# A decoder trunk's MLP on one core: the first product as seven half-size products per block instead of eight

## The chip, the core and the metric

The kernel runs on one core of a Trainium2 chip. A time is the time of one execution on the device in microseconds (us), the median of several runs. Engines are named as in the profile: PE does matrix products, PEld loads their weights, DVE and ACT are the vector and scalar engines, POOL a slower third one, and SP issues the transfers (DMA) between DRAM and the on-chip memory.

## The reference: what is computed

One layer of a decoder trunk on 512 tokens with 2048 features: three parallel token mixers, merged by gates, an output projection, and an MLP. Only the last part matters here.

```python
D_MODEL = 2048; SEQ = 512; D_FF = 4 * D_MODEL
x = x + merged @ w_out                       # output projection, residual
h = rmsnorm(x, norm_mlp)                     # y * rsqrt(mean(x*x) + 1e-6) * g
x = x + jnp.square(jax.nn.relu(h @ mlp_w1)) @ mlp_w2   # (512 x 2048)(2048 x 8192), then (512 x 8192)(8192 x 2048)
out = rmsnorm(x, final_norm)
```

All products are wanted with the accuracy of 32-bit floats.

## The kernel before

Activations lie feature-major: a tile has 128 features on the partitions and the 512 tokens along the row. Each operand of a big product is split into a high and a low part (`hl`: ACT rounds a copy to the type fp32r, DVE subtracts it), and a product of two tiles is three matrix instructions: high by high, high by low, low by high. `gemm` does one output tile of 128 features: it calls `wtiles` for each slab of up to eight weight tiles (128 x 1024 numbers, 512 KB), which issues the load, ACT's cast and DVE's subtraction; raw slabs have 3 buffers (`wraw`), high and low parts 3 each (`whl`), and a slab's high and low parts are free again when PE has used the slab.

The order on PE is that of the code; the other engines and the queue SP are ordered by a scheduler, and each works its list strictly in order. Everything is read as one stream on PE:

- the mixers and the gates, up to 1471 us of the trace;
- the output projection `wo`: 16 output tiles, each 16 weight tiles x 3 instructions. For each, DVE adds the product to the residual `x1`, and ACT and DVE make `hh` and `ho`, the scaled high and low parts that the first MLP product reads;
- the MLP in 8 rounds `c`. A round makes 8 output tiles of the first product (`w1_{f}`, 16 weight tiles x 3 instructions of 512 columns each), whose result goes through ReLU, the factor `R` (one over the rms) and a square into `ah`, `al`; then 16 output tiles of the second product over these 8 tiles (`w2_{c}_{j}`, 8 x 3 instructions), each added to `x1[j]` by DVE;
- the last eight tiles of the last round are done in two halves of the tokens, in instructions of 256 columns, and the final norm follows for each half.

The psum banks of these products are a ring of two (`gps`, tag "g", `gb = 2`): the third product begins when the first one's bank has been read. Products into other banks use a ring of six (`ps`).

## Time and profile before

| | |
|---|---|
| median of 3 runs | 3062.77 us (3061.63 to 3068.74) |
| profiled execution | span 3059.8 us, first to last instruction; its own time is not listed beside it, and the span lies 2.97 below the median of the runs |
| PE busy | 3001.3 us, 98% of the span |
| DVE, ACT, POOL busy | 1557.3, 989.0, 336.8 us |
| data moved | 370.72 MB, mean 121 GB/s |
| `wo`, first to last instruction | 1471.7 to 1645.5 us |
| MLP up to the halves of the tokens | 1645.7 to 2995.6 us |

"Busy" of PE counts each matrix instruction from its start to its end, and these overlap, so the mean length of an instruction is not what one costs in a stream: that is the distance between the starts of neighbours. Idle time is that just before an instruction, with what released it.

### The profile page before, as it was taken

The page shows a single profiled execution, that of the slowest core. Times are in us where ns is not written, and L with a number is a line of the kernel's source. Part 1 is how long each engine was busy: PE and PEld are TensorE (multiplying, and loading weights), DVE is VectorE, ACT ScalarE, POOL GpSimd, SP SyncE. Part 2 cuts the span into 40 slices and gives each one's busy share as a digit, 9 for nine tenths or more (in the row PEclk, how much of TensorE's full clock was granted, in tenths as well). Part 3 has the DMA queues.
Part 4 walks back from the last instruction along what each step waited for, and adds up shares of the span by engine and source line. Part 5 has one row for each costly group of instructions (what it writes and reads, how often), then busy time and mean ns, then how long its engine had stood idle before and what let it go on. Part 6 is the DMA issues. An engine that isn't in the chain of part 4 may idle for free.

```text
span 3059.8 us, 36455 instructions
## 1 busy us (share of the span) xinstructions
PE 3001.3 (98%) x14143; PEld 2468.2 (81%) x14143; DVE 1557.3 (51%) x2350; ACT 989.0 (32%) x1224; POOL 336.8 (11%) x572
## 2 busy tenths in 40 slices
PE   8999988999999999999999999999999999999997
PEld 7888776788877777888888888888888888888887
DVE  7766888855664555555334334333333434333335
ACT  6554121234662233422223222122222212222235
POOL 1001766530000000011110000000000000000003
PEclk9999988999999999999999999999999999999999
DMA  5345333445337163655432333333233323323334
GB/s 181 124 162 185 114 103 98 136 131 166 102 103 190 55 186 97 229 165 170 157 98 94 97 99 96 99 98 97 97 97 97 97 96 97 97 96 97 97 97 151
DMA packets 172638, 370.72 MB, mean 121 GB/s; under 512 B 63377, under 2 KB 74385, under 8 KB 171665
## 3 DMA queue, kind: packets, MB, share of 16 engines
q1 hardware_dynamic: 172464, 368.38, 38.2%
q8 instruction: 112, 1.84, 0.3%
q14 instruction: 62, 0.50, 0.1%
HBM read 318.81 MB, written 44.58 MB: 119 GB/s over the span
## 4 chain that ended last, share of the span: by engine, by line
PE 85%; DVE 6%; POOL 3%; DMA 3%; SPq 1%; issue 1%; ACT 0%; DVEq 0%; ACTq 0%; POOLq 0%
PE w L748 15%; PE w L749 15%; PE w L750 15%; PE gt L748 5%; PE gt L750 5%; PE gt L749 5%; PE z L748 2%; PE z L750 2%; PE z L749 2%; PE wo L750 2%; PE up L748 2%; PE wo L748 2%; PE up L750 2%; PE up L749 2%; PE wo L749 2%
## 5 line engine op out<-in xcount | busy, mean ns | idle before, releaser
L731 ACT CAST whw<-wrw 128x1024 fp32r<-128x1024 f32 x264 | 278.0, 1053 | 885.8 <-PE w L749 872.4
L32 DVE TENSOR_TENSOR wlw<-wrw,whw 128x1024 fp32r<-128x1024 f32 x264 | 324.1, 1227 | 405.2 <-ACT whw L731 405.2
L748 PE MATMUL w<-ah,whw 128*128 128x512 f32 (+1 forms) x1088 | 409.9, 377 | 0.1
L750 PE MATMUL w<-ah,wlw 128*128 128x512 f32 (+1 forms) x1088 | 409.7, 377 | 0.0
L749 PE MATMUL w<-al,whw 128*128 128x512 f32 (+1 forms) x1088 | 409.7, 377 | 0.0
L748 PE MATMUL w<-hh,whw 128*128 128x512 f32 x1024 | 398.7, 389 | 0.0
L750 PE MATMUL w<-hh,wlw 128*128 128x512 f32 x1024 | 398.4, 389 | 0.0
L749 PE MATMUL w<-ho,whw 128*128 128x512 f32 x1024 | 398.4, 389 | 0.0
L748 PE MATMUL gt<-uh,whgt 128*128 128x512 f32 x768 | 310.6, 404 | 2.8 <-DVE gz L26 2.8
L750 PE MATMUL gt<-uh,wlgt 128*128 128x512 f32 x768 | 300.6, 391 | 2.0 <-DVE wlgt L32 2.0
L749 PE MATMUL gt<-ul,whgt 128*128 128x512 f32 x768 | 300.2, 391 | 0.0
L29 DVE TENSOR_TENSOR x<-x,w 128x512 f32<-128x512 f32 (+1 forms) x136 | 89.2, 656 | 388.0 <-PE w L750 388.0
L748 PE MATMUL z<-uh,whin 128*128 128x512 f32 x608 | 243.7, 401 | 11.8 <-DVE zs L26 11.8
L750 PE MATMUL z<-uh,wlin 128*128 128x512 f32 x608 | 241.0, 396 | 8.1 <-DVE wlin L32 8.1
L749 PE MATMUL z<-ul,whin 128*128 128x512 f32 x608 | 240.0, 395 | 0.0
L748 PEld LDWEIGHTS w<-ah,whw 128*128 128x128 f32 x1088 | 204.7, 188 | 37.7 <-issue 0.2
L749 PEld LDWEIGHTS w<-al,whw 128*128 128x128 f32 x1088 | 204.7, 188 | 37.5
L750 PEld LDWEIGHTS w<-ah,wlw 128*128 128x128 f32 x1088 | 204.7, 188 | 37.4
L748 PEld LDWEIGHTS w<-hh,whw 128*128 128x128 f32 x1024 | 192.2, 188 | 40.2 <-issue 0.2
L749 PEld LDWEIGHTS w<-ho,whw 128*128 128x128 f32 x1024 | 192.2, 188 | 40.1 <-issue 0.2
L750 PEld LDWEIGHTS w<-hh,wlw 128*128 128x128 f32 x1024 | 192.2, 188 | 39.9
L29 POOL TENSOR_TENSOR acc<-acc,sq 128x512 f32<-128x512 f32 x29 | 49.7, 1713 | 1521.7 <-ACT sq L830 1490.7
(442 smaller groups left out, 4577.8 us busy)
## 6 DMA issues: line engine op xcount, KB each, us to landing
wrw<-in_w SPq DMA_DIRECT2D x264, 512.0 KB, 3.6
wrgt<-in_w_in SPq DMA_DIRECT2D x96, 512.0 KB, 4.0
wrin<-in_w_in SPq DMA_DIRECT2D x76, 512.0 KB, 3.6
wrup<-in_w_up SPq DMA_DIRECT2D x32, 512.0 KB, 4.0
wrwo<-in_w_out SPq DMA_DIRECT2D x32, 512.0 KB, 3.6
gd<-gz SPq DMA_DIRECT2D x48, 256.0 KB, 2.2
gl<-gd SPq DMA_DIRECT2D x48, 256.0 KB, 3.1
zd<-zs SPq DMA_DIRECT2D x21, 256.0 KB, 2.0
```

Of the source, the lines that this page charges most:

```text
L29: (eng or self.nc.vector).tensor_tensor(out, a, b, ALU.add)
L32: (eng or self.nc.vector).tensor_tensor(out, a, b, ALU.subtract)
L731: nc.scalar.copy(hi, raw)
L748: nc.tensor.matmul(ps, hi[:, ws], xh, start=first, stop=False)
L749: nc.tensor.matmul(ps, hi[:, ws], xl, start=False, stop=False)
L750: nc.tensor.matmul(ps, lo[:, ws], xh, start=False, stop=last)
```

## The change

The first MLP product is cut in 32 units `u` of 256 output features, and each unit is a 2 x 2 block product: two halves of the 2048 input features (8 tiles each), two output tiles, two halves of the tokens (256). Of such a block product the change computes seven products of sums instead of eight (the Strassen-Winograd form): each of the seven is 8 weight tiles x 3 instructions of 256 columns. Their inputs are sums of the two feature halves and the two token halves, made once and kept per product (`hA` for products 1, 5, 6, 3, made by `hsums` while `wo` runs; three more, `hB`, that go to DRAM as `d3` and are read back and split at the start of the first unit). The weights' sums are made per unit by `wsums`: 5 loads of 512 KB, 4 additions on DVE, and a cast and a subtraction for each of the 7. `w1_out` copies three partial results from psum, makes the four quarters of the block, applies ReLU, square and the factor, and stores the 512 KB to DRAM (`hid`). The second product is as before, but it begins after the last unit, reads its activations back (`hidden`), and takes `x1` from DRAM too (`x1d`, stored during `wo`). `R2` is now 1/(mean + 1e-6), multiplied after the square.

```diff
+    ORDER = (1, 5, 6, 3, 7, 2, 4)
+    BANK = {1: "a", 6: "a", 7: "a", 4: "a", 5: "c", 3: "c", 2: "b"}
...
+    def wsums(self, name, B, pool):
+        nc = self.nc
+        at = {}
+        def load(c, q):
+            p = pool if c == "A" else None
+            at[c] = (p or self.wp).tile([P, 1024], F32, name=f"w{c}{name}", tag="wA" if p else "wraw", bufs=self.wA if p else self.wraw)
+            nc.sync.dma_start(at[c], B[q])
+            return at[c]
+        def acc(c, t):
+            self.add(at[c], at[c], t)
+            return at[c]
+        how = {1: lambda: load("A", "11"), 5: lambda: acc("A", load("D", "12")), 6: lambda: acc("A", load("B", "22")),
+               3: lambda: at["B"], 7: lambda: acc("B", load("E", "12")), 2: lambda: load("C", "21"), 4: lambda: acc("A", at["C"])}
+        for i in self.ORDER:
+            with self.tc.high_priority(self.wprio):
+                x = how[i]()
+                hi, lo = (self.wp.tile([P, 1024], F32R, name=f"w{q[0]}{name}_{i}", tag="w" + q, bufs=self.whl) for q in ("hi", "lo"))
+                nc.scalar.copy(hi, x)
+                self.sub(lo, x, hi)
+            yield i, hi, lo
+    def w1_mm(self, ps, i, w, hc, ks):
+        for k in ks:
+            ws = slice(k * P, k * P + P)
+            for q, (a, b) in enumerate(((0, 0), (0, 1), (1, 0))):
+                self.nc.tensor.matmul(ps, w[a][:, ws], hc[i][b][:, k], start=i in (1, 5, 2) and k == 0 and q == 0,
+                                      stop=k == 7 and q == 2, skip_group_check=True)
+    def w1_out(self, u, i, bank, keep, pool, R2, hid):
+        nc = self.nc
+        with self.tc.high_priority(2 * self.wprio):
+            if i in (1, 5, 6):
+                keep[i] = pool.tile([P, 256], F32, name=f"pk{i}_{u}", tag=f"pk{i}", bufs=2)
+                nc.scalar.copy(keep[i], bank[self.BANK[i]])
+            if i == 1:
+                keep["y"] = pool.tile([P, 4, 256], F32, name=f"hy{u}", tag="hy", bufs=2)
+            y = keep["y"]
+            if i == 7:
+                self.sub(y[:, 2], keep[5], bank["a"])
+            elif i == 2:
+                self.add(y[:, 1], bank["b"], keep[1])
+            elif i == 3:
+                self.sub(y[:, 3], bank["c"], keep[6])
+            elif i == 4:
+                nc.scalar.copy(y[:, 0], bank["a"])
+                f = y.rearrange("p q t -> p (q t)")
+                nc.scalar.activation(f, f, AF.Relu)
+                nc.scalar.activation(f, f, AF.Square)
+                v = y.rearrange("p (h q) t -> p h (q t)", h=2)
+                self.mul(v, v, R2.unsqueeze(1).broadcast_to([P, 2, T]))
+                nc.sync.dma_start(hid[u], f)
...
+        self.wraw, self.whl, self.wA = 3, 3, 4
...
+                HA = (1, 5, 6, 3)
+                upper, front = contextlib.ExitStack(), contextlib.ExitStack()
+                hp = upper.enter_context(mixpool("hcu", "right"))
+                hA = [hp.tile([P, 8, 4, 256], F32R, name=f"hA{q}") for q in "hl"]
+                hc = {i: [t[:, :, n] for t in hA] for n, i in enumerate(HA)}
+                fp = front.enter_context(mixpool("front", "right"))
+                x1d = [dr.tile([P, T], F32, name=f"x1d{j}") for j in range(NT)]
+                d3 = dr.tile([P, 3, 8, 256], F32, name="d3")
+                acc = R
+                x1 = {}
+                def residual(n, j):
+                    x1[j] = fp.tile([P, T], F32, name=f"x1_{j}", tag="x1", bufs=4)
+                    nc.sync.dma_start(x1[j], d["xT"][j])
+                    pt = self.gps(f"wo{j}")
+                    self.run(self.gemm(f"wo{j}", d["w_out"][j], [(pt, NT)], m))
+                    with tc.high_priority(self.wprio):
+                        self.add(x1[j], x1[j], pt)
+                    self.sumsq(acc, x1[j], n)
+                    nc.sync.dma_start(x1d[j], x1[j])
+                def hsums(k):
+                    with tc.high_priority(self.wprio):
+                        G = fp.tile([P, 7, 256], F32, name=f"hG{k}", tag="hG")
+                        for q, c in enumerate((0, 4)):
+                            nc.scalar.activation(G[:, c:c + 2].rearrange("p q t -> p (q t)"), x1[k + 8 * q], AF.Copy,
+                                                 scale=col("norm_mlp", k + 8 * q))
+                        a21, a11, s1, s2, a22, a12, s4 = (G[:, q] for q in range(7))
+                        self.sub(s1, a21, a22)
+                        self.sub(s2, s1, a11)
+                        self.add(s4, s2, a12)
+                        self.sub(a21, a11, a21)
+                        for o, g in ((0, slice(1, 4)), (3, slice(6, 7))):
+                            n = g.stop - g.start
+                            hi, lo = (t[:, k, o:o + n] for t in hA)
+                            nc.scalar.copy(hi, G[:, g])
+                            self.sub(lo, G[:, g], hi)
+                        nc.sync.dma_start(d3[:, 0, k], a21)
+                        nc.sync.dma_start(d3[:, 1, k], a12)
+                        nc.sync.dma_start(d3[:, 2, k], a22)
+                seq = [q for k in range(8) for q in (k, k + 8)]
+                for n, j in enumerate(seq):
+                    residual(n, j)
+                    if n % 2:
+                        hsums(j - 8)
+                trunk.close()
...
+                gen = self.wsums("u0", w1_quadrants(0), None)
+                bank, keep = banks(0), {}
+                two = [next(gen) for _ in range(2)]
+                for i, *w in two:
+                    self.w1_mm(bank[self.BANK[i]], i, w, hc, range(7))
+                front.close()
+                for i, *w in two:
+                    self.w1_mm(bank[self.BANK[i]], i, w, hc, range(7, 8))
+                    self.w1_out(0, i, bank, keep, mp, R2, hid)
+                wA = side.enter_context(mixpool("wA", "right"))
+                with mixpool("hraw", "right") as rp:
+                    for n, i in ((2, 4), (1, 2), (0, 7)):
+                        hc[i] = [mp.tile([P, 8, 256], F32R, name=f"hB{i}{q}") for q in "hl"]
+                    for n, i in enumerate((7, 2, 4)):
+                        with tc.high_priority(self.wprio):
+                            for h in range(2):
+                                t = rp.tile([P, 4, 256], F32, name=f"hraw{i}{h}", tag="hraw", bufs=3)
+                                nc.sync.dma_start(t, d3[:, n, 4 * h:4 * h + 4])
+                                self.hl(t, *(q[:, 4 * h:4 * h + 4] for q in hc[i]))
+                    for n, (i, *w) in enumerate(gen):
+                        self.w1_mm(bank[self.BANK[i]], i, w, hc, range(8))
+                        self.w1_out(0, i, bank, keep, mp, R2, hid)
+                        if n == 1:
+                            pm = self.gps("pms")
+                            nc.tensor.matmul(pm, self.onesD, acc, start=True, stop=True)
+                            self.ts(R2, pm, 1e-6, ALU.add)
+                            nc.vector.reciprocal(R2, R2)
+                for u in range(1, 32):
+                    bank, keep = banks(u), {}
+                    for i, *w in self.wsums(f"u{u}", w1_quadrants(u), wA):
+                        self.w1_mm(bank[self.BANK[i]], i, w, hc, range(8))
+                        self.w1_out(u, i, bank, keep, mp, R2, hid)
+                side.close()
...
+                    def hidden(u):
+                        with tc.high_priority(2 * self.wprio):
+                            t = rp.tile([P, 1024], F32, name=f"hr{u}", tag="hr", bufs=3)
+                            nc.sync.dma_start(t, hid[u])
+                            r = [xp.tile([P, 1024], F32R, name=f"a{q}{u}", tag=f"a{q}", bufs=8) for q in "hl"]
+                            self.hl(t, *r)
+                        return [tuple(x[:, T * q:T * q + T] for x in r) for q in range(2)]
+                    nxt = [a for u in range(4) for a in hidden(u)]
+                    xq = [mp.tile([P, 4, T], F32, name=f"x1b{j}") for j in range(NT // 4)]
...
+                        nc.sync.dma_start(x1[j], x1d[j])
...
-                        aa = []
-                        for q in range(8):
-                            f = 8 * c + q
-                            pt = self.gps(f"w1_{f}") if f else pw
-                            if f:
-                                self.run(self.gemm(f"w1_{f}", d["w1"][f], [(pt, NT)], hh))
-                            t = stg.tile([P, T], F32, name=f"a{f}", tag="z")
-                            nc.scalar.activation(t, pt, AF.Relu)
-                            self.mul(t, t, R)
-                            self.mul(t, t, t)
-                            hi = ap.tile([P, T], F32R, name=f"ah{f}", tag="act")
-                            lo = ap.tile([P, T], F32R, name=f"al{f}", tag="act")
-                            self.hl(t, hi, lo)
-                            aa.append((hi, lo))
+                        aa, nxt = nxt, []
...
+                            if c < 7 and j in (2, 4, 6, 8):
+                                nxt += hidden(4 * c + 3 + j // 2)
```

What follows are rows of the engines' lists, without times; a tile's name is followed by its number. First PE in the middle of the first product, before: output tile `w1_1`, the activations `hh`/`ho` and the weights' parts `wh`/`wl`.

```order
L748 MATMUL w1_1_13530<-hh0_12412,whw1_1_0_13533 128x512
L749 MATMUL w1_1_13530<-ho0_12413,whw1_1_0_13533 128x512
L750 MATMUL w1_1_13530<-hh0_12412,wlw1_1_0_13534 128x512
L748 MATMUL w1_1_13530<-hh1_12479,whw1_1_0_13533 128x512
L749 MATMUL w1_1_13530<-ho1_12480,whw1_1_0_13533 128x512
L750 MATMUL w1_1_13530<-hh1_12479,wlw1_1_0_13534 128x512
```

and now, unit 10, product 1, with the first kept input `hA` and the parts of the unit's weight sum.

```order
L802 MATMUL ha10_15920<-hAh_12340,whu10_1_15925 128x256
L802 MATMUL ha10_15920<-hAl_12341,whu10_1_15925 128x256
L802 MATMUL ha10_15920<-hAh_12340,wlu10_1_15926 128x256
L802 MATMUL ha10_15920<-hAh_12340,whu10_1_15925 128x256
L802 MATMUL ha10_15920<-hAl_12341,whu10_1_15925 128x256
L802 MATMUL ha10_15920<-hAh_12340,wlu10_1_15926 128x256
```

Each instruction has half the columns, and each still has a weight tile of its own; the product before is 3072 rows of the first kind, the product now 5376 of the second. Next the queue SP at the start of the first product, before (`wr` are raw weights):

```order
L728 DMA wrw1_0_0_13453<-in_w1 128x1024
L728 DMA wrw1_0_8_13491<-in_w1 128x1024
L728 DMA wrw1_1_0_13531<-in_w1 128x1024
L728 DMA wrw1_1_8_13561<-in_w1 128x1024
L728 DMA wrw1_2_0_13600<-in_w1 128x1024
L728 DMA wrw1_2_8_13630<-in_w1 128x1024
```

and now (`hraw` are the three inputs read back, with the product's number and a half; `wAu1` to `wAu4` the first quarters of later units, `wCu0` the quarter that products 2 and 4 of unit 0 need):

```order
L1225 DMA d3_12361<-hG7_13546 128x256
L1264 DMA hraw70_13680<-d3_12361 128x1024
L1264 DMA hraw71_13684<-d3_12361 128x1024
L1264 DMA hraw20_13688<-d3_12361 128x1024
L781 DMA wAu1_13871<-in_w1 128x1024
L781 DMA wAu2_14099<-in_w1 128x1024
L781 DMA wAu3_14327<-in_w1 128x1024
L781 DMA wAu4_14555<-in_w1 128x1024
L781 DMA wCu0_13802<-in_w1 128x1024
L1264 DMA hraw21_13692<-d3_12361 128x1024
L1264 DMA hraw40_13696<-d3_12361 128x1024
L781 DMA wDu1_13904<-in_w1 128x1024
```

Nine 512-KB transfers stand here behind the last store of `d3`; `hraw41` is the next row. Last, DVE at the beginning of the second product, before, with the first addition into `x1`:

```order
L32 TENSOR_TENSOR wlw2_0_2_0_14081<-wrw2_0_2_0_14078,whw2_0_2_0_14080 128x1024
L26 TENSOR_TENSOR a7_14005<-a7_14005,R_81 128x512
L26 TENSOR_TENSOR a7_14005<-a7_14005 128x512
L32 TENSOR_TENSOR al7_14010<-a7_14005,ah7_14009 128x512
L29 TENSOR_TENSOR x1_0_12340<-x1_0_12340,w2_0_0_14013 128x512
```

and now (`hr` the activations read back, `x1b` the tiles of `x1` that are read back):

```order
L33 TENSOR_TENSOR al7_21314<-hr7_21311,ah7_21313 128x1024
L33 TENSOR_TENSOR wlw2_0_3_0_21111<-wrw2_0_3_0_21108,whw2_0_3_0_21110 128x1024
L33 TENSOR_TENSOR wlw2_0_4_0_21143<-wrw2_0_4_0_21140,whw2_0_4_0_21142 128x1024
L30 TENSOR_TENSOR x1b0_20985<-x1b0_20985,w2_0_0_21005 128x512
L30 TENSOR_TENSOR x1b0_20985<-x1b0_20985,w2_0_1_21006 128x512
```

with the rows of SP that bring `x1b` in:

```order
L1298 DMA hr10_21777<-hid10_13576 128x1024
L729 DMA wrw2_0_6_0_21210<-in_w2 128x1024
L1306 DMA x1b0_20985<-x1d0_12345 128x512
L1306 DMA x1b0_20985<-x1d1_12346 128x512
L729 DMA wrw2_0_7_0_21248<-in_w2 128x1024
L1306 DMA x1b0_20985<-x1d2_12347 128x512
```

The first addition now stands behind the parts of two later slabs, and its `x1b` behind the seventh slab of the second product in the queue, which takes the raw buffer of the fourth (`w2_0_3`).

## Rows read from the trace of the kernel before

**Rows 1.** The page's busy times of the engines over the span.
```profile
span 3059.8 us, 36455 instructions
PE 3001.3 (98%) x14143; PEld 2468.2 (81%) x14143; DVE 1557.3 (51%) x2350; ACT 989.0 (32%) x1224; POOL 336.8 (11%) x572
```

**Rows 2.** Waits of PE from 1500 us on: total, times, longest (us).
```profile
engine line waited for: us in total, times, longest us
PE pn L819 <- ACT sq L1196: 0.5, 1, 0.5
```

**Rows 3.** Groups by line and form, PE: instructions, busy us, mean ns, idle.
```profile
L748 PE MATMUL w<-hh,whw 128*128 128x512 f32 x1024 | 398.7, 389 | 0.0
L748 PE MATMUL w<-ah,whw 128*128 128x256 f32 x128 | 36.5, 285 | 0.1
```

**Rows 4.** Timeline of PE, first product: start us, length us; 96 starts apart.
```profile
2899.67 0.39 PE L750 MATMUL w<-hh,wlw 128*128 128x512 f32 x1
...
2921.43 0.39 PE L750 MATMUL w<-hh,wlw 128*128 128x512 f32 x1
```

**Rows 5.** Timeline of PE, second product in halves; 60 starts apart.
```profile
2995.77 0.28 PE L748 MATMUL w<-ah,whw 128*128 128x256 f32 x1
...
3002.97 0.28 PE L748 MATMUL w<-ah,whw 128*128 128x256 f32 x1
```

**Rows 6.** Timeline of the weight loads in the same halves.
```profile
2996.01 0.19 PEld L748 LDWEIGHTS w<-ah,whw 128*128 128x128 f32 x1
2996.13 0.19 PEld L749 LDWEIGHTS w<-al,whw 128*128 128x128 f32 x1
```

**Rows 7.** Groups by line and form, DVE and ACT.
```profile
L32 DVE TENSOR_TENSOR wlw<-wrw,whw 128x1024 fp32r<-128x1024 f32 x264 | 324.1, 1227 | 405.2 <-ACT whw L731 405.2
L29 DVE TENSOR_TENSOR x<-x,w 128x512 f32<-128x512 f32 x120 | 82.5, 688 | 382.7 <-PE w L750 382.7
L29 DVE TENSOR_TENSOR x<-x,w 128x256 f32<-128x256 f32 x16 | 6.7, 418 | 5.2 <-PE w L750 5.2
L731 ACT CAST whw<-wrw 128x1024 fp32r<-128x1024 f32 x264 | 278.0, 1053 | 885.8 <-PE w L749 872.4 <-PE wo L749 8.8 <-issue 4.6
L304 ACT COPY s5ys<-s5y 128x256 f32<-128x256 f32 x12 | 4.4, 369 | 26.0 <-PE s5y L302 19.3 <-DMA wrin<-in_w_in 6.7
```

**Rows 8.** Timeline, all engines: how soon ACT and DVE follow a release.
```profile
2799.48 0.39 PE L749 MATMUL w<-al,whw 128*128 128x512 f32 x1
...
2799.91 1.05 ACT L731 CAST whw<-wrw 128x1024 fp32r<-128x1024 f32 x1 [4.34 <-PE w L749]
...
2800.99 1.23 DVE L32 TENSOR_TENSOR wlw<-wrw,whw 128x1024 fp32r<-128x1024 f32 x1 [0.17 <-ACT whw L731]
```

**Rows 9.** Transfers: count, KB each, median us from issue to landing.
```profile
wrw<-in_w SPq DMA_DIRECT2D x264, 512.0 KB, 3.6
gd<-gz SPq DMA_DIRECT2D x48, 256.0 KB, 2.2
s5mat<-in_s5mat SPq DMA_DIRECT2D x12, 128.0 KB, 2.1
```

**Rows 10.** Stretches with dense loads: five engines' busy us, PEclk, DMA share, GB/s.
```profile
20.00:25.00 5.00, 5.00 (x24) 4.14 (x23) 5.00 (x8) 4.23 (x7) 0.00 (x0) 1.00 1.03 381
```

**Rows 11.** The one reciprocal on DVE: ns min/median/max, form.
```profile
L171 DVE RECIPROCAL s5s<-s5s x1: 453/453/453, 57.2 to 57.2; 128x48 f32<-128x48 f32 x1
```

**Rows 12.** Two stretches of PE about a long gap: busy us, PEclk, DMA share, GB/s.
```profile
380.00:390.00 10.00, 2.62 (x12) 0.81 0.09 26
390.00:400.00 10.00, 9.26 (x31) 0.68 0.58 175
```

**Rows 13.** Timeline of PE at a short gap.
```profile
42.62 0.39 PE L750 MATMUL z<-uh,wlin 128*128 128x512 f32 x1
45.39 1.12 PE L817 MATMUL pn<-acc,cst 128*128 128x512 f32 x2 [2.38 <-DVE acc L29]
```

More of the change, by code (lines that the diff above doesn't have):

```diff
@@ L1 @@
+import contextlib
 import math
@@ L842, in main @@
         self.w1, self.w2, self.w3, self.w4 = 14, 4, 18, 28
-        self.wraw, self.whl = 3, 3
+        self.wraw, self.whl, self.wA = 3, 3, 4
         self.gb, self.psb = 2, 6
@@ new lines, in main @@
+                seq = [q for k in range(8) for q in (k, k + 8)]
[4 more added lines that the diff above has]
+                trunk.close()
+                lower, side = contextlib.ExitStack(), contextlib.ExitStack()
+                mp = lower.enter_context(mixpool("w1"))
+                R2 = mp.tile([P, T], F32, name="R2")
+                hid = [dr.tile([P, 1024], F32, name=f"hid{u}") for u in range(32)]
@@ new lines, in w1_quadrants, with banks @@
+                def w1_quadrants(u):
+                    w = d["w1"]
+                    return {f"{k + 1}{n + 1}": w[2 * u + n][:, 1024 * k:1024 * k + 1024] for k in range(2) for n in range(2)}
+                def banks(u):
+                    return {q: self.ps(f"h{q}{u}")[:, 0:256] for q in "acb"}
+                gen = self.wsums("u0", w1_quadrants(0), None)
[3 more added lines that the diff above has]
+                    self.w1_mm(bank[self.BANK[i]], i, w, hc, range(7))
@@ new lines, in main @@
+                for u in range(1, 32):
[4 more added lines that the diff above has]
+                side.close()
+                upper.close()
+                lower.close()
+                with contextlib.ExitStack() as st:
+                    mp, hp = (st.enter_context(mixpool(n)) for n in ("x1b", "nrm"))
+                    self.stg = st.enter_context(tc.tile_pool(name="sq", bufs=3, reuse_waits="tile"))
+                    sq2 = hp.tile([P, T], F32, name="sq2")
+                    gap = st.enter_context(mixpool("gap"))
+                    gap.tile([P, 20 * 256], F32, name="gap")
+                    rp = st.enter_context(mixpool("hr"))
+                    xp = st.enter_context(mixpool("ah", "right"))
+                    acc2 = hp.tile([P, T], F32, name="acc2")
+                    tmp = hp.tile([P, T], F32, name="rt1")
+                    def hidden(u):
[7 more added lines that the diff above has]
+                    xq = [mp.tile([P, 4, T], F32, name=f"x1b{j}") for j in range(NT // 4)]
+                    x1 = [xq[j // 4][:, j % 4] for j in range(NT)]
+                    for j in range(NT):
+                        nc.sync.dma_start(x1[j], x1d[j])
+                    for c in range(8):
+                        aa, nxt = nxt, []
@@ L1181, in main @@
                     fin = None
-                    sq2 = mp.tile([P, T], F32, name="sq2")
                     for h in range(2):
@@ L1210, in main @@
                     fin()
+            banks8.close()
 _RW = ("w0", "a0", "k_k", "k_a", "r_k", "lnx_w", "lnx_b")
```

38 lines of the change are left out of this document (6 added, 32 removed).

## The prediction

> **What bounds the kernel now.** I read the page first: PE is busy for 98% of the span [rows 1], the other engines for half of theirs or less. Then the waits of PE from 1500 us on: one of 0.5 us [rows 2], so through `wo` and the MLP nothing but PE's own pace counts, and a wait that the change brings there is paid in full. Then the groups by form: the mean length, 389 ns for 512 columns, 285 for 256 [rows 3], would make half the columns cost 73%, and seven halves for four wholes a clear loss. But the instructions overlap. The timeline shows the starts: 96 in 21.76 us, 0.2267 us apart, at 512 columns [rows 4]; 60 in 7.20 us, 0.1200 apart, at 256 [rows 5]. That is the price in a stream: 213.3 ns for the 256 more columns twice over, and 13.3 fixed per instruction. The halves of the second product are the very form that the change uses, with a new weight tile for each instruction.
>
> **What the change removes and adds on PE.** Before, 64 tiles x 16 x 3 = 3072 instructions x 0.2267 = 696.4 us. Now 32 units x 7 x 8 x 3 = 5376 x 0.1200 = 645.1. **-51.3 us**, not the eighth of 696 (87) that seven for eight promises: the fixed 13.3 ns is paid 5376 times instead of 3072.
>
> The skill speaks against it. The Trainium skill, "TensorE: Matmul & The Clock Gate", Part 3 (what overlaps and what doesn't), says that a weight load overlaps a running product only when it goes to other row groups, and here each takes all rows. Here loads of 0.19 us start 0.12 apart [rows 6], so they overlap each other and the products; by the rule they would be in series (a rival below).
>
> **Does a unit keep PE fed?** A unit is 168 x 0.120 = 20.16 us of PE, a product 2.88. ACT: 7 casts x 1.053, four copies of 256 from psum x 0.37, ReLU and square of 1024 taken like a cast, 1.05 each: 11.0 us. DVE: 12 operations on 1024 x 1.23 and three on 256 x 0.42: 16.0 [rows 7]. Both fit, but each list is in order, and DVE waits for ACT in each product. I walked the lists with these lengths and 0.04 us per release: ACT follows a product's end by that (2799.87 to 2799.91), and DVE the cast [rows 8]. The tightest place is product 7. ACT's cast for it stands behind the copy of product 6 out of psum, so from the start of 6's last instruction: its length 0.28, copy 0.37, cast 1.05, DVE's low part 1.23, three releases: 3.05 us. PE wants the low part at its third instruction: 0.12 x 27 = 3.24. Everywhere else there is a microsecond or more: the load D of the next unit is issued when 7's low part is done, lands 3.6 us later [rows 9] and is wanted 1.8 after that. Bounds: 0, or if a release costs 0.15 rather than 0.04, about 0.15 x 31 = 5; I take **+2**, nearer to the measured release. Bandwidth is no limit: 3.1 MB in 20.2 us is 156 GB/s, and 381 have been moved [rows 10].
>
> `wo` itself: per pair of tiles `hsums` brings DVE 4 x 0.42 and two low parts, ACT two casts, in place of the old `hh`, `ho`; 9 us of DVE in 21.8 of PE. The new stores wait in SP for the end of a tile, but the slabs behind them are wanted 20 us later. Nothing. If that cover were gone, each pair would show 1 to 2 us, 16 at most. The extra traffic (32 MB of `hid`, 8 of `x1`) lies beside PE for the same reason.
>
> **The first unit.** Count from the end of `wo` (0). PE runs the first 7 tiles of products 1 and 5: 42 x 0.12 = 5.0. The sums of the last tile pass DVE and ACT by 5.6 (add 0.69, a cast that stands ahead, scale 0.72, the subtractions, casts, low parts); then 6 more instructions, products 6 and 3 and the norm's, to 13. Product 7 needs `hB7`. `d3`'s last store is issued at 4.5, lands after 2.1 [rows 9], 6.6; the first reload lands 3.6 later, 10.2, and each of the 512 KB behind it 1.4 later (524 KB at 381 GB/s [rows 10]). In the queue `wCu0` is eighth: 20.0; `hraw40` tenth: 22.8; `hraw41` twelfth: 25.6. Product 7: two halves through ACT and DVE, copy of 6, its own weights: starts at 15.3, ends 18.2. Product 2 waits for `wCu0`, 20.0. DVE by then has the factor's reciprocal: 0.453 us for 48 columns [rows 11], for 512 between 0.7 (as any operation) and 4.8 (by the column); I take 4.3. With it DVE is free for the addition of `wCu0` at 22.4, then low part 24.9, second half of `hB2`, parts for product 4 and the next unit, `hB4` at 29.8 and 31.0, 1.23 each: product 2 ends at 27.8, product 4 at 32.7. Without stalls 20.2: 12.5 lost (10.2 if the reciprocal is cheap). The gaps, up to some 6 us about product 2, can lower the clock: before, a gap of 2.4 us left it [rows 13], one of over 7 cost 3.2 us in the stretch behind (0.68 of 10 us [rows 12]). I add 1.5: **+14**, bounds 10 and, if the twelve transfers don't overlap at all (3.6 each, the last at 50), 38.
>
> **From first to second product.** The activations of round 0 are long in DRAM; their parts are made in the last three products. Count from the end of product 4 of unit 31. `w2_0_0` and `w2_0_1` run side by side; the first ends at 9.5, the second at 10.9. The third takes the first's bank (ring of two), which DVE reads when `x1b` has come. That stands in SP behind the slab `w2_0_6`, which takes the raw buffer of `w2_0_3`, free when DVE has its low part, whose buffer `w2_0_0` held until 9.5: cast to 10.8, low part 12.0, issue, 3.6 to land plus 0.7 for the 256 KB behind it: 16.4, addition 0.69: 17.1. Before, this addition had its `x1` in place. **PE waits 6.2 us**, the second addition follows at once, after that the tiles come faster (0.7) than PE asks (5.4). The clock after such a gap: 2.5, between 0 and 3.2. Together **+9**, bounds 5 and 13. Later rounds have their `hid` half a round ahead.
>
> **The sum**, against the span: -51.3 + 2 + 14 + 9 = -26. 3059.8 - 26 = 3033.5; the runs' median lies 3.0 above the span, so **3036 us**, 0.9% less.
>
> **Rivals.**
> - The handovers cost far more: transfers of the first unit come in series (38 instead of 14): -51.3 + 38 + 9 + 2 = -2, 3060. For it: 512-KB loads take 3.6 us each [rows 9]. Against: the dense stretches moved 381 GB/s [rows 10]. No change.
> - They cost little: the reciprocal is cheap, `x1b` comes while the bank is not yet asked for, no clock is lost: -51.3 + 10 = 3021 and below.
> - Slower: the units don't keep up. Place: ACT and DVE in turn, in order. If no cast lies beside DVE's work a unit takes 16.0 + 7 x 1.05 = 23.3 instead of 20.16: +98, 3132. It decides from 0.8 us per unit (26 / 31). Against: the walk, and DVE's additions that stand between cast and low part.
> - The weight load bounds: 5376 x 0.188 = 1011 us instead of 645, +366: 3400. Rows 6 and 5 contradict it directly, unless the 23 us in which the form was seen are a special case [rows 5, 6].
> - That seven for eight isn't done: excluded, the list has 2304 rows more on PE, 5376 - 3072.
>
> **How the numbers follow.** A difference of 0.3%, 9 us, is about what a measurement of this kernel tells from none. Forecast 0.60 (its own range 3024 to 3050: reciprocal and clock at their bounds, +2 at 0 or 5), handovers cheaper 0.10, far dearer 0.13, units behind 0.14, weight loads 0.03. Faster: 0.60 + 0.10 + 0.03 of the dearer; same: the other 0.10 and 0.03 of units slightly behind; slower 0.14. The range must leave out no more than 0.2: from 3017, half of the cheap case, to 3062, the dear case's end.
>
> **What the profile after would show.** Starts 0.120 apart in products `ha`, `hb`, `hc`, and a unit from 30 on 20.2 to 20.4 long; a wait of PE for DVE or ACT at product 7's low part of 0 to 0.2; in unit 0 waits of 2 to 7 us at products 7, 2 and 4, for `hB` and `wCu0`; one wait of 6 us at `w2_0_2` for DVE's addition, with the granted clock below 1 behind it; 98% of PE's time elsewhere as before. The prediction is wrong if the unit is 21 or longer, if the starts are further apart than 0.12, or if waits stand in `wo` or the later rounds.

## The result

The changed kernel takes 3032.8 us (median of 4 runs, 3031.3 to 3033.5), the kernel before beside it 3064.7 (4 runs, 3061.6 to 3068.7): ratio 0.9894, 95% interval 0.9880 to 0.9908. The 3036 predicted lie 3 us off. The profiled executions differ by 3059.8 - 3030.8 = 29.0 us.

The page's busy times after the change, which answer to [rows 1]:

```profile
span 3030.8 us, 42091 instructions
PE 2957.9 (98%) x16447; PEld 2523.5 (83%) x16447; DVE 1828.9 (60%) x2578; ACT 1161.0 (38%) x1434; POOL 329.0 (11%) x572
```

PE is still the bound, with 2304 more instructions and 43 us less of busy time. Its waits from 1470 us on, where there was one of 0.5 us before [rows 2]:

```profile
engine line waited for: us in total, times, longest us
PE w L749 <- DVE x1b L30: 8.2, 2, 8.1
PE hb L802 <- ACT whu L793: 2.6, 1, 2.6
PE ha L802 <- ACT pk L811: 2.3, 2, 1.4
PE hb L802 <- DVE wlu L33: 2.0, 1, 2.0
```

They are the two handovers that the prediction named: `x1b` ahead of `w2_0_2`, and unit 0. Five stretches of the changed kernel (length; PE, PEld, DVE, ACT, POOL busy with instructions; granted clock; DMA share; GB/s) are unit 0, units 1 to 31, the handover in two pieces, and the second product behind it:

```profile
1648.00:1679.00 31.00, 23.24 (x166) 21.16 (x166) 26.24 (x26) 15.17 (x19) 1.45 (x1) 0.94 0.73 259
1679.00:2285.00 606.00, 606.00 (x5216) 605.96 (x5215) 478.63 (x470) 327.92 (x408) 0.00 (x0) 1.00 0.49 163
...
2295.00:2305.00 10.00, 1.92 (x7) 1.27 (x7) 4.62 (x5) 1.88 (x2) 0.00 (x0) 0.75 0.97 373
2305.00:2315.00 10.00, 10.00 (x34) 7.96 (x33) 1.90 (x2) 1.05 (x1) 0.00 (x0) 0.74 0.94 344
2320.00:2960.00 640.00, 640.00 (x2744) 516.70 (x2743) 246.04 (x253) 152.82 (x150) 7.81 (x5) 1.00 0.34 111
```

The second row is the first surprise: PE never waits in 31 units, and 606.00 us hold 5216 instructions, 0.1162 us each and not 0.1200. The last is the second: 640.00 / 2744 is 0.2332 for 512 columns, and not the 0.2267 of [rows 4]. The timeline of PE shows where (start, length): in unit 2, 21 starts on `hA`, then 21 on `hB2`; in the second product, 96 starts at 512 columns.

```profile
1702.16 0.28 PE L802 MATMUL hc<-hAh,whu 128*128 128x256 f32 x1
...
1704.54 0.28 PE L802 MATMUL hc<-hAh,whu 128*128 128x256 f32 x1
...
1713.18 0.28 PE L802 MATMUL hb<-hB2h,whu 128*128 128x256 f32 x1
...
1715.70 0.28 PE L802 MATMUL hb<-hB2h,whu 128*128 128x256 f32 x1
...
2699.84 0.39 PE L749 MATMUL w<-ah,whw 128*128 128x512 f32 x1
...
2722.24 0.39 PE L749 MATMUL w<-ah,whw 128*128 128x512 f32 x1
```

2.38 / 21 = 0.1133 on `hA`, 2.52 / 21 = 0.1200 on `hB`, 22.40 / 96 = 0.2333 in the second product. The instructions of the second product and their shapes are those of before; only their tiles lie elsewhere.

The accounts of the two profiled executions, from the starts of PE's instructions:

| term | predicted, us | measured, us |
|---|---|---|
| first product at its own pace (3072 x 0.1133 + 2304 x 0.1200 = 624.6 for 696.4) | -51.3 | -71.8 |
| waits inside units 1 to 31 | +2 | 0 |
| unit 0 (31.46 for 19.52) | +14 | +11.9 |
| handover to the second product (8.1 of wait and the clock behind it) | +9 | +10.9 |
| second product at 0.2333, 2880 instructions; its halves | 0 | +19.2; -1.1 |
| ahead of `wo`, not touched by the change | 0 | +2.5 |
| sum | -26 | -28.4 of 29.0 |

The 2.5 us ahead of `wo` are of the size by which executions differ there: in the profiled ones of the changed kernel and its variants below, `wo` begins anywhere from 1469.4 to 1476.5.

So the total came out right over two errors of 20 us that cancel. The experiments are about these two first, then about the handovers.

### The profile page after: what moved, and what is told of

The parts are those of the page before. It is cut to its first block, busy times and chain, and to the rows that moved or that the text cites. A ratio compares the mean times of both kernels' runs of the same rounds, so it can differ in the third digit from the quotient of the medians.

```text
span 3030.8 us, 42091 instructions
## 1 busy us (share of the span) xinstructions
PE 2957.9 (98%) x16447; PEld 2523.5 (83%) x16447; DVE 1828.9 (60%) x2578; ACT 1161.0 (38%) x1434; POOL 329.0 (11%) x572
## 4 chain that ended last, share of the span: by engine, by line
PE 84%; DVE 6%; POOL 3%; DMA 3%; issue 2%; SPq 1%; ACT 1%; DVEq 0%; ACTq 0%; POOLq 0%
PE ha L802 12%; PE w L749 8%; PE w L750 8%; PE w L751 8%; PE hc L802 6%; PE gt L749 5%; PE gt L751 5%; PE gt L750 5%; PE hb L802 3%; PE z L749 2%; PE z L751 2%; PE z L750 2%; PE wo L750 2%; PE up L751 2%; PE up L750 2%; PE wo L749 2%
## 5 line engine op out<-in xcount | busy, mean ns | idle before, releaser
L732 ACT CAST whw<-wrw 128x1024 fp32r<-128x1024 f32 x136 | 143.2, 1053 | 505.9 <-PE w L750 504.3
L30 DVE TENSOR_TENSOR x1b<-x1b,w 128x512 f32<-128x512 f32 (+1 forms) x136 | 89.2, 656 | 394.7 <-PE w L751 389.6
L732 ACT CAST whgt<-wrgt 128x1024 fp32r<-128x1024 f32 x96 | 100.3, 1046 | 269.6 <-PE gt L750 168.5
L793 ACT CAST whu<-wAu 128x1024 fp32r<-128x1024 f32 x128 | 133.8, 1046 | 159.9 <-DVE wAu L30 83.2
L33 DVE TENSOR_TENSOR wlu<-wAu,whu 128x1024 fp32r<-128x1024 f32 x128 | 156.4, 1222 | 44.9 <-ACT whu L793 44.9
L33 DVE TENSOR_TENSOR wlw<-wrw,whw 128x1024 fp32r<-128x1024 f32 x136 | 167.3, 1230 | 21.9 <-ACT whw L732 21.9
L749 PEld LDWEIGHTS gt<-uh,whgt 128*128 128x128 f32 x768 | 144.4, 188 | 37.7 <-issue 4.1
L751 PEld LDWEIGHTS gt<-uh,wlgt 128*128 128x128 f32 x768 | 144.6, 188 | 34.7 <-DVE wlgt L33 3.2
L30 POOL TENSOR_TENSOR acc<-acc,sq 128x512 f32<-128x512 f32 x14 | 23.0, 1642 | 1338.2 <-ACT sq L896 1308.0
L750 PEld LDWEIGHTS gt<-ul,whgt 128*128 128x128 f32 x768 | 144.9, 189 | 27.1
```

Source lines behind the costliest of these rows:

```text
L30: (eng or self.nc.vector).tensor_tensor(out, a, b, ALU.add)
L33: (eng or self.nc.vector).tensor_tensor(out, a, b, ALU.subtract)
L732: nc.scalar.copy(hi, raw)
L749: nc.tensor.matmul(ps, hi[:, ws], xh, start=first, stop=False)
L750: nc.tensor.matmul(ps, hi[:, ws], xl, start=False, stop=False)
L751: nc.tensor.matmul(ps, lo[:, ws], xh, start=False, stop=last)
```

## The experiments

The theory after the result: the fixed part of an instruction, 6.7, 13.3 or 20 ns here, depends on where the moving tile lies in SBUF. Rivals: the traffic beside PE; alignment to 64 bytes. In the built program the weights' tiles lie at 32 bytes modulo 256 (43296, 55584), `hB` too (82208), `hA` and `ah` at 224 (163808), which is 192 bytes off.

**micro_place.** A kernel of its own; a cell is:

```
for k in range(8):
    for q, (a, b) in enumerate(((wh, mh), (wh, ml), (wl, mh))):
        nc.tensor.matmul(ps[0][:, 0:n], at(a + 512 * k, 128), at(b + step * k, n),
                         start=k == 0 and q == 0, stop=k == 7 and q == 2)
```

> Only a stream of matmuls on an otherwise idle core (nothing of the reference is computed; the output is filler): 120 cells of 24 instructions with 256 or 512 columns, weights and moving tile at chosen addresses, the last matmul of 64 columns of each cell marks its end. In the changed kernel the products on hA start 0.1133 us apart, those on hB 0.1200, and w2 now 0.2333 instead of 0.2267, with no wait. Theory A (the place in SBUF of the moving tile sets the fixed part): the cells at hA's place show 0.113, at hB's 0.120, with 512 columns at the right side's place 0.233 and at the left side's 0.227. Theory B (the traffic of the other engines and of the DMA beside it sets it): all cells of one width are alike, the 256 ones at or below 0.113, the 512 ones at or below 0.227. Theory C (the step of 32 bytes off a 64-byte line): the cells shifted by -32 are 0.0067 shorter than their neighbours.

The timeline, first cells: `hB`'s place, then `hA`'s with steps of 4096 and of 2048 bytes (the length is that of the 24 together):

```profile
69.12 3.12 PE L71 MATMUL w<-big 128*128 128x256 f32 x24
...
72.11 3.07 PE L71 MATMUL w<-big 128*128 128x256 f32 x24
...
75.05 2.99 PE L71 MATMUL w<-big 128*128 128x256 f32 x24
```

Mean starts 0.1200, 0.1177 and 0.1135, and with 512 columns 0.2272, 0.2333, 0.2333, with nothing beside PE: theory B falls. A, as it stood, falls as well: 18 places 8 KB apart, from 72 to 208 KB, all give 0.1196, and with 512 columns 0.2272 or 0.2273. They have one thing in common, 32 modulo 256, the weights' own. Shifting only the moving tile by -32 bytes took `hB`'s cell from 0.1200 to 0.1180 but `hA`'s from 0.1135 to 0.1173; shifting weights and tile together gave 0.1196 and 0.1133 again. So it is their distance, theory D: d is the moving tile's address less the weights', modulo 256 bytes, 0 for `hB` and 192 for `hA`.

This holds in steps of 32 bytes. Cells 16 bytes off show that d is not all: with 512 columns and d = 16, starts were 0.2316 apart where the moving tile had been shifted and 0.2284 where the weights had been. These are the two cells:

```profile
292.42 5.81 PE L71 MATMUL w<-big 128*128 128x512 f32 x24
...
315.23 5.74 PE L71 MATMUL w<-big 128*128 128x512 f32 x24
```

Nor is `hA`'s cell at one price: with the changed kernel's own step of 4096 it showed 0.1177 and not that kernel's 0.1133, and the next cell, with the same step and d, 0.1133.

**a_shift32.** In the changed kernel:

```diff
+            cp.tile([P, 8], F32, name="pad")
...
+                rpad.tile([P, 8], F32, name="rpad")
                 hp = upper.enter_context(mixpool("hcu", "right"))
```

> The changed kernel with everything in SBUF behind the constants moved up by 32 bytes and everything on the right side moved down by 32 bytes; no instruction changes. Theory C (every matmul operand lies 32 bytes off a 64-byte line and pays 16 cycles for it): the spacing falls by 0.0067 us everywhere, units by 168 x 0.0067 = 1.1 us, the run by 60 to 90 us, to about 2950. Theories A and B: same within 0.3%, spacings 0.113, 0.120 and 0.233 stay.

3046.0 us (4 runs, 3044.3 to 3048.7), ratio to before 0.9939 (0.9922 to 0.9955): slower than the changed kernel by 13, and none of the three theories had that. C falls. By D it is plain: left and right moved apart, so `hA` and `ah` went from 192 to 128 bytes off the weights.

```profile
L802 PE MATMUL ha<-hAl,whu 128*128 128x256 f32 x480 | 135.0, 281 | 0.0
...
L751 PE MATMUL w<-ah,wlw 128*128 128x512 f32 x790 | 311.7, 395 | 0.0
```

Mean lengths (the same groups) were 277 and 396 in the changed kernel: the starts on `hA` are now 0.1186 apart, a unit 20.01 us, 31 x 0.48 = +15; the second product 0.2324, 2880 x -0.0010 = -3.

**micro_offset.** The same kernel, cells of 48 instructions:

```
for rep in range(3):
    for n in (256, 512):
        for w in (32, 96):
            for d in range(0, 256, 32) if rep != 1 else range(224, -1, -32):
                cell(n, d, w)
```

> Again only a stream of matmuls on an idle core (nothing of the reference is computed). 96 cells of 48 instructions: 256 or 512 columns, the weights at two places 64 bytes apart, the moving tiles d bytes off the weights' place modulo 256, d from 0 to 224 in steps of 32, three times over (the second time backwards). Theory D (it is the distance of the moving tile from the weights modulo 256 bytes that sets the fixed part): d = 0 shows 0.120 and 0.227, d = 192 shows 0.113 and 0.233, the same for both places of the weights and in each repetition; the other d lie between 0.113 and 0.120, and between 0.227 and 0.237. Rival (it is chance, or what ran before): a cell's three repetitions and two places differ among themselves as much as the d do.

Timeline, 256 columns at d = 0, at 192 and at 192 the second time round; 512 columns at d = 0 and 192:

```profile
68.18 6.00 PE L57 MATMUL w<-big 128*128 128x256 f32 x48
...
102.75 5.70 PE L57 MATMUL w<-big 128*128 128x256 f32 x48
...
346.08 5.90 PE L57 MATMUL w<-big 128*128 128x256 f32 x48
...
160.27 11.17 PE L57 MATMUL w<-big 128*128 128x512 f32 x48
...
227.65 11.45 PE L57 MATMUL w<-big 128*128 128x512 f32 x48
```

Mean distance of the starts in ns, least and greatest of three repetitions and both places of the weights:

| d, bytes | 0 | 32 | 64 | 96 | 128 | 160 | 192 | 224 |
|---|---|---|---|---|---|---|---|---|
| 256 columns | 119.8, 120.0 | 116.7, 117.8 | 113.3, 117.8 | 119.7, 120.0 | 118.6, 118.7 | 117.3, 118.7 | 113.3, 117.8 | 118.2, 118.4 |
| 512 columns | 226.7, 227.4 | 233.3, 233.4 | 228.9, 229.1 | 233.2, 233.6 | 232.2, 233.3 | 234.1, 234.4 | 233.3, 233.3 | 233.3, 233.3 |

At 512 columns D holds: for one d, places and repetitions differ by 1.1 ns at most, and the d by 7.7. Best there is d = 0, which with 96 is the worst for 256. At 256 columns D holds for d = 0, 96, 128 and 224 (0.3 ns or less); at 32 the two places of the weights differ (116.7 and 117.8 in each repetition), at 160 one cell of six stands 1.3 ns off, and at 64 and 192 there are two levels, 113.3 and 117.8, two thirds of the whole range apart. There the rival is right: at 192 all cells of the backward pass took the upper level, those of the two forward passes the lower, so it hangs on what ran before. At 64 the cells with the weights at 32 did the same, those with the weights at 96 took the upper each time.

**b_halves.** The kernel before, with the halves alone:

```diff
+                    if name.startswith("w1"):
+                        nc.tensor.matmul(ps[:, 0:256], w[:, ws], x[:, 0:256], start=f, stop=False, skip_group_check=True)
+                        nc.tensor.matmul(ps[:, 256:512], w[:, ws], x[:, 256:512], start=False, stop=l, skip_group_check=True)
```

> The kernel before, its first MLP product with eight products but each instruction of 512 columns cut into two of 256 (the halves alone, without seven for eight): 6144 instructions of 256 columns on tiles of the left side. By the fixed 13.3 ns that the prediction took for the form: 6144 x 0.1200 = 737.3 instead of 696.4, +41 us, 3105. If the fixed part is 6.7 ns as on hA: 6144 x 0.1133 = 696.3, no change. If the weight load bound it: 6144 x 0.188 = 1155, +459 us.

3104.8 us (4 runs), +39.6 beside its own runs of before (3065.2), ratio 1.0129 (1.0114 to 1.0144). The first product takes 737.6 us, 0.1200 each: the prediction's price of a half, for tiles at d = 0, is right, and halves there without seven for eight cost 41 us.

**a_banks.** In the changed kernel:

```diff
-                        if n == 1:
+                        if n == 3:
                             pm = self.gps("pms")
...
+                        bank8 = self.gps if c else self.ps
+                        pts = [bank8(f"w2_{c}_{j}") for j in range(2)]
...
+                                pt = bank8(f"w2_{c}_{j}")
```

> The changed kernel with two waits taken away: round 0 of the second product takes its psum tiles from the six banks that the first product has left, so that w2_0_2 need not wait for the addition to x1b_0; and the norm's product and the reciprocal in unit 0 come after product 2 instead of after product 3. Prediction's theory (the wait for x1b at the bank and the lower clock behind it are lost time): the wait of 8.1 us and about 2.5 us of clock are gone; and without the 3.35 us of the reciprocal ahead of wCu0's addition, unit 0 is 2 us shorter: 3020, -12 us. Rival: the wait only moves (the additions pile up behind x1b's loads and PE waits when the banks are used up, or for the slabs behind it): less than 3 us gained.

3024.1 us (4 runs, 3022.1 to 3025.8), ratio 0.9866 (0.9852 to 0.9881). The windows at the handover, against 1.92 us of work and a clock of 0.75 above:

```profile
2295.00:2305.00 10.00, 10.00 (x45) 8.01 (x44) 5.71 (x5) 4.52 (x5) 0.00 (x0) 1.00 0.97 344
2305.00:2315.00 10.00, 10.00 (x45) 8.01 (x44) 5.02 (x6) 1.73 (x2) 0.00 (x0) 1.00 1.04 392
```

From the second product's first start to PE's last end it is 719.4 us for 730.7: wait and clock behind it cost 11 us together, and both are gone. The other half missed: unit 0 went from 31.5 to 33.3. Its waits fell by a microsecond (7.8 to 6.9), but the granted clock over 1648 to 1680 is 0.84, where it was 0.94 to 1679.

**a_c0.** In the changed kernel:

```diff
+                if early and i == 6:
+                    at["C"] = early.tile([P, 4, 256], F32, name="wC0", tag="hy", bufs=2).rearrange("p q t -> p (q t)")
+                    nc.sync.dma_start(at["C"], B["21"])
```

> The changed kernel with wCu0, the weights of product 2 of the first unit, in a buffer of its own (the second one of hy, idle in unit 0) and so issued ahead of the reloads of hraw. The prediction's step (product 2 of unit 0 waits for wCu0's landing and then for the addition behind the reciprocal): the waits of 2.6 and 2.0 us before and in product 2 go, unit 0 falls from 31.5 to 27 us, -4 us, about 3029. Rival (the reloads hraw21 and hraw40 are as late, and wCu0 only gives its wait to them): unit 0 stays within 1 us of 31.5.

3029.4 us (4 runs, 3025.5 to 3036.2), unit 0 30.2 where 27 was expected: nearer to the rival. (Of the 7.4 us by which the profiled execution is shorter, 4.8 lie ahead of `wo`.) PE's longest waits there are now

```profile
PE hb L806 <- DVE hB2l L33: 2.4, 1, 2.4
PE ha L806 <- DVE hAl L33: 1.4, 1, 1.4
```

for the reload `hraw21` (at `hB2`) and for `hA`'s last low part, where it was 0.6.

**a_place.** In the changed kernel:

```diff
+                mp.tile([P, 48], F32, name="bpad")
                 with mixpool("hraw", "right") as rp:
...
+                    st.enter_context(mixpool("apad", "right")).tile([P, 48], F32, name="apad")
                     xp = st.enter_context(mixpool("ah", "right"))
```

> The changed kernel with two tiles of 192 bytes that nothing uses: one moves the hidden activations of the second product (ah, al) to the weights' place modulo 256 bytes, as in the kernel before, the other moves hB7, hB2, hB4 to 192 bytes off it, as hA lies. No instruction changes. Theory D (the distance modulo 256 sets the fixed part): w2's spacing falls from 0.2333 to 0.2267, 2880 x 0.0067 = -19 us; hB's falls from 0.120 to 0.113 or 0.1178, 2304 x 0.0067 = -15 us or 2304 x 0.0022 = -5 us; together -24 to -34, some 3000 to 3009. Rival (in the whole kernel the other engines' accesses set it): spacings as they were, no change.

2999.4, 3004.8, 3022.9 and 3027.9 us: all faster than the changed kernel, but 28 us apart. In the profiled one (2999.4) `hA` and `hB` both run at 0.1133, units 2 to 30 take 19.04 us, and behind the handover the second product's starts are 0.2267 apart: D in the whole kernel. A new wait costs part of it back, for the first `ah`:

```profile
PE w L749 <- ACT ah L876: 11.1, 1, 11.1
```

**a_best32, a_best192.** The edits of a_banks (without the moved reciprocal), a_c0 and a_place, with `ah`'s 192 bytes taken from under `hA`:

```diff
+                upper.enter_context(mixpool("hpad", "right")).tile([P, 48], F32, name="hpad")
```

> The changed kernel with what the runs pointed to: the six free banks for round 0 of the second product, wCu0 in its own buffer, ah and al at the weights' place modulo 256 (their 192 bytes taken from under hA, so that no tile of wA lies in their way), and hB 32 bytes off it, where 256 columns took 0.1167 each time. Theory D: 3032.8 - 11.3 (banks) - 1.2 (wCu0) - 19.2 (w2) - 31 x 72 x 0.0033 = 7.4 (hB) = 2994, with little spread between executions. Rival (the offsets' levels do not hold when hA and hB follow each other at different ones): hA leaves 0.1133 for 0.1178, +13, 3007.

> As a_best32, but hB 192 bytes off the weights' place, as hA. Theory D with its two levels at 192 bytes: when all products run at 0.1133, 3032.8 - 11.3 - 1.2 - 19.2 - 31 x 72 x 0.0067 = 14.9 gives 2986; when all run at 0.1178, 31 x 168 x 0.0045 = 23 more, 3009; executions spread between the two. Rival: one level holds, spread within 4 us as with the changed kernel itself.

3013.1 us (5 runs, 3010.8 to 3016.0) and 3004.3 (4 runs, 2999.9 to 3008.0), ratios 0.9835 and 0.9807. The levels hold: `hA` 0.1133 and `hB` 0.1167 in the one, 0.1133 throughout units 1 to 31 in the profiled execution of the other. That execution is the slowest of its four (3008.0), so their spread of 8 us is not that of the levels. `wCu0`'s own buffer gained nothing here: unit 0 takes 32.5 and 34.3 us, for 31.5 in the changed kernel. And both wait 11.0 us for the first `ah`, so the wait was not `wA`'s:

```profile
2286.03 0.79 PE L749 MATMUL w<-ah,whw 128*128 128x512 f32 x1 [11.04 <-ACT ah L880]
```

ACT's cast stood idle for `hr`, whose loads were issued at 2280.1 in a_best192, 5 us behind the end of unit 31 on PE; in the changed kernel they were issued 4.6 us ahead of it. By the layout in SBUF, `pk6` with 32 or 192 bytes more ahead of it reaches into the place of `hr`; a_final tests this.

**a_final.** a_best192 without a_c0's edit, and

```diff
-                    gap.tile([P, 20 * 256], F32, name="gap")
+                    gap.tile([P, 20 * 256 + 48], F32, name="gap")
```

> a_best192 without wCu0's own buffer (it gave its wait to the reloads) and with 192 bytes more in the tile gap, so that hr, as in the changed kernel, lies clear of pk6: in a_best192 the loads hr waited for the end of unit 31, and PE 11.0 us for the first ah. Theory: that wait and the clock behind it (3.5 us) go, the rest stays: 3004 - 11 - 3.5 = 2990, 2986 to 2993 at the lower of the two levels of 192 bytes, up to 3013 at the upper. Rival (the wait was the pads' on the right side, not hr's): 11 us of wait stay, 3004.

The wait is gone, and the second product's 2880 instructions take 652.8 us, exactly as before the change. Six executions: 2986.8, 2987.0, 2989.7 and 3012.1, 3013.9, 3016.5; median 3000.9, ratio 0.9792 (0.9759 to 0.9825). The profiled one is of the upper group, by groups of form from 1700 to 2285 us:

```profile
L802 PE MATMUL ha<-hAl,whu 128*128 128x256 f32 x480 | 134.9, 281 | 0.0
```

281 ns and 0.1178 apart, against 277 and 0.1133. 31 x 168 x 0.0045 = 23 us is nearly the distance of the groups (26). The lower group of this kernel has no profile; that it is the level 0.1133, as in the profiled executions of a_place and a_best192, is likely and not shown. But this execution holds both levels. Up to product 7 of unit 1 the starts are 0.1133 apart. Then one step takes 0.16 us, at the first instruction with the low part, the place that the prediction called the tightest, and from there on they are 0.1178 apart. In product 4 of unit 31 a step of 0.18 us leads back to 0.1133:

```profile
1691.16 0.28 PE L802 MATMUL ha<-hB7h,whu 128*128 128x256 f32 x1
1691.27 0.28 PE L802 MATMUL ha<-hB7l,whu 128*128 128x256 f32 x1
1691.39 0.33 PE L802 MATMUL ha<-hB7h,wlu 128*128 128x256 f32 x1
1691.55 0.28 PE L802 MATMUL ha<-hB7h,whu 128*128 128x256 f32 x1
1691.67 0.28 PE L802 MATMUL ha<-hB7l,whu 128*128 128x256 f32 x1
1691.79 0.28 PE L802 MATMUL ha<-hB7h,wlu 128*128 128x256 f32 x1
...
2290.45 0.34 PE L802 MATMUL ha<-hB4h,whu 128*128 128x256 f32 x1
2290.63 0.28 PE L802 MATMUL ha<-hB4l,whu 128*128 128x256 f32 x1
```

Not every such break changes the level: one of 0.22 us at the same place of a_place left it at 0.1133. Every one of the six is faster than every execution of the changed kernel.

**a_front.** a_final with the four loads `wAu1` to `wAu4` behind unit 0's own in the queue:

```diff
-                wA = side.enter_context(mixpool("wA", "right"))
...
+                wA = side.enter_context(mixpool("wA", "right"))
                 for u in range(1, 32):
```

> a_final with the pool of the four wA tiles opened behind the reloads' pool and over its place, so that in unit 0 the loads wAu1 to wAu4 (2.1 MB) stand in SP's queue behind wCu0, hraw21, hraw40 and hraw41 instead of ahead of them. The prediction's step (in unit 0 product 2 waits for what stands eighth, tenth and twelfth in the queue): 2.1 MB at the 400 GB/s of that stretch are 5.2 us, unit 0 falls from 31 to about 26 us, and less clock is lost: 5 us less than a_final. Rival (DVE's and ACT's work, with the reciprocal's 3.35 us in it, holds unit 0): unit 0 within 1.5 us of a_final's.

3004.6 us (6 runs, 2990.6 to 3015.8), no gain. Unit 0 took 30.8 us, a_final's 32.4; unit 1 took 23.0, a_final's 19.4. Windows of a_front, then of a_final:

```profile
1680.00:1700.00 20.00, 17.94 (x145) 17.05 (x144) 15.90 (x16) 10.44 (x13) 0.00 (x0) 1.00 0.60 200
```

```profile
1680.00:1700.00 20.00, 20.00 (x175) 20.00 (x175) 16.47 (x16) 10.70 (x15) 0.00 (x0) 1.00 0.57 201
```

The queue's order only says which unit pays.

**a_slack.** In the changed kernel:

```diff
-                nc.scalar.copy(keep[i], bank[self.BANK[i]])
+                for _ in range(2 if i == 6 else 1):
+                    nc.scalar.copy(keep[i], bank[self.BANK[i]])
```

> The changed kernel with product 6's copy out of psum made twice (same value), 0.37 us more on ACT ahead of the cast for product 7, the place that the prediction called the tightest. The prediction's walk: 3.05 us of chain against the low part wanted 24 x 0.1133 + 2 x 0.120 + 0.12 = 3.08 after product 6 begins its last instruction: no room, so 0.3 us of wait in each of 31 units, +10 us, 3043, and the wait shows at the low part of product 7. Rival (the chain has a microsecond of room, since ACT runs ahead): no wait and no change, 3033.

3042.0 us (4 runs, 3040.2 to 3045.8), +9 on the changed kernel; units 1 to 31 take 617.6 us for 605.3. The timeline at product 7:

```profile
1808.57 0.27 PE L802 MATMUL ha<-hB7l,whu 128*128 128x256 f32 x1
1808.97 0.38 PE L802 MATMUL ha<-hB7h,wlu 128*128 128x256 f32 x1
1809.20 0.28 PE L802 MATMUL ha<-hB7h,whu 128*128 128x256 f32 x1
```

The low part's first instruction starts 0.40 behind its neighbour instead of 0.12, the next 0.23 behind that, in every unit. The list of waits doesn't name it: the modelled end of an instruction (0.27 after its start) hides most of so short a gap; the starts show it. So the walk of the lists is right to a tenth of a microsecond: 0.37 us more, and 0.40 us longer units. The changed kernel has no room left there. The run shows something of the levels too: in unit 1 a break moved `hA`'s products 6 and 3 to 0.1178, and behind `hB`'s three products at d = 0 unit 2 was at 0.1133 again.

## Why the prediction was right

**The pace of PE.** This is the step that was mis-sized: "the fixed 13.3 ns is paid 5376 times". I read one price for 256 columns in one place [rows 5] and took it for the form's. It is that of tiles at d = 0: it held for `hB` (0.1200) and in b_halves, not for `hA` at d = 192 (0.1133). The term is -71.8, not -51.3.

**The second product was taken as unchanged**, as the change says of it. Its instructions are, but `ah` and `al` moved from d = 0 to 192, and 2880 x 0.0067 = 19.2 us came back. a_final, with the tiles at d = 0, takes the 652.8 us of before. These two errors cancel by chance: that the total is right to 3 us was luck, and it proved nothing about its terms.

**Units keep PE fed.** +2 for a late low part of product 7: 0 measured, with a_slack showing that the place is the right one and that it is just wide enough. The first stall was less than a tenth of a microsecond away; the rival "the units don't keep up" needed 0.8 us per unit, and a_slack's 0.37 us more cost 9 us in all.

**The first unit.** Its times are right stage by stage, from the end of `wo` at 1648.27: product 7 begins at 15.8 (15.3 predicted), product 2 ends at 28.1 (27.8), product 4 at 31.5 (32.7). DVE's rows, start and length:

```profile
1666.38 3.35 DVE L1273 RECIPROCAL R<-R 128x512 f32<-128x512 f32 x1
1669.65 0.36 DVE L33 TENSOR_TENSOR hy<-pk,ha 128x256 f32<-128x256 f32 x1
1669.93 1.21 DVE L30 TENSOR_TENSOR wAu<-wAu,wCu 128x1024 f32<-128x1024 f32 x1
1671.06 1.22 DVE L33 TENSOR_TENSOR wlu<-wCu,whu 128x1024 fp32r<-128x1024 f32 x1
```

The reciprocal took 3.35, of the 0.7 to 4.8 that 48 columns [rows 11] allowed. What the runs don't support is that a single late item holds the unit. Moving the reciprocal, the late `wCu0` or the loads ahead of the reloads changed it by +1.8, -1.2 and -1.6, and where it gained most, unit 1 lost 3.6. All that the unit needs comes in one block behind `wo`; what bounds it as a whole was not isolated.

**The handover.** Forecast 6.2 of wait and 2.5 of clock, measured 8.1 and, with a_banks, 11 together. The mechanism (bank, addition, `x1b` behind the slab `w2_0_6`) is shown by the row that ends the wait:

```profile
2304.47 0.77 PE L749 MATMUL w<-ah,whw 128*128 128x512 f32 x1 [8.08 <-DVE x1b L30]
```

The mis-sized part is the landing of `x1b`: issued at 2297.5, its addition began at 2303.6, 6.1 us for the 4.3 that I took from a quieter queue [rows 9]; the stretch moved 373 GB/s.

**Weight loads in series** had 0.03 and fell: loads of 0.19 us start 0.113 apart, and b_halves cost 40 us more, not 459. The Trainium skill, "TensorE: Matmul & The Clock Gate", Part 3 (what overlaps and what doesn't), lets a load overlap a running product only on other row groups. That does not hold for this stream, where each load takes all rows:

```profile
1702.84 0.19 PEld L802 LDWEIGHTS hc<-hAl,whu 128*128 128x128 f32 x1
1702.95 0.19 PEld L802 LDWEIGHTS hc<-hAh,wlu 128*128 128x128 f32 x1
```

## What to carry to other kernels

Where PE is the bound, a change that moves tiles changes the price of instructions that it does not touch: read the distance of the starts by tile, before and after, and look at the places modulo 256 bytes. A price per instruction that is read from one stream is one of several, so give it a range; here 13.3 ns would have been 6.7 to 20. What cutting the columns costs hangs on the place as well: at d = 0 it was a loss by itself (+41 us) that only the work saved pays for, while at d = 192 two starts at 0.1133 take less than one at 0.2333 (not run in a kernel). And a handover costs more than its wait: free psum banks took 8 us of wait away and 3 of clock with it.

## What the runs showed that I had not expected

The start-to-start time of a matmul on whole 128 x 128 weights hangs on the distance of its moving tile from its weights modulo 256 bytes: from 0.1133 (d = 64, 192) to 0.1200 (d = 0, 96) at 256 columns, from 0.2267 (d = 0) to 0.2344 (d = 160) at 512. The Trainium skill, "TensorE: Matmul & The Clock Gate", Back-to-back issue gap, gives N / 2.4 + 2.5 ns for N columns as the gap of an isolated matmul, and 131 ns at 512 columns for a stream of weight loads and matmuls. The streams here are of the second kind and measured neither: N / 2.4 + 6.7 at the least with 256 columns, 226.7 ns at the least with 512.

At d = 192 (and 64) the same stream runs at one of two levels, 0.1133 or 0.1178. In a_final's trace it changes only at a break in the stream, and without one the upper level lasts for some 30 units. Its six times lie in two groups 26 us apart, as if executions differed in this. The changed kernel, whose `hA` follows `hB` at d = 0 in each unit, stayed at the lower level in its profile and within 2.2 us in its four runs, and a_slack came back to it within a unit. Which break changes the level, and whether the weights' and the moving tile's reads disturb each other, as the dependence on their distance suggests, was not tried; a_best32 without its 11 us of wait, the steadier version, was not run.
